# A two-block layer on one core: block products of a triangular inversion in separate bursts, transfers handed out when their data are there, low maps first, two output units begun early

## The chip, the cores and the metric

The kernel runs on one core of a Trainium2 chip. The metric is the device time of one execution in microseconds (us); smaller is better. Engines: PE = TensorE matmul, PEld = TensorE weight load, DVE = VectorE, ACT = ScalarE, POOL = GpSimd, SP = SyncE, which issues most transfers.

## The reference

Two transformer-like blocks over 512 tokens of width 1024. The change touches the mixer of the second block alone: an RWKV-7 recurrence and a gated depthwise convolution of 31 taps, each followed by an output map and merged by two gates. Cut to that:

```python
def rwkv7_time_mix(h, p_r, p_k, p_v, ...):
    xx = token_shift(h) - h
    r, k, v = (lerp_shift(p, mu) for p, mu in zip((p_r, p_k, p_v), mu_rkv))
    w_log = -softplus(-(w0 + tanh((h + xx * mu_wag[0]) @ w1) @ w2)) - 0.5
    decay = exp(-exp(w_log))
    a = sigmoid(a0 + ((h + xx * mu_wag[1]) @ a1) @ a2)
    g = sigmoid((h + xx * mu_wag[2]) @ g1) @ g2
    kk = heads(k * kk_scale) / norm                     # 16 heads of 64
    y = wkv7(r, decay, k * (1 + (a - 1) * ka_scale), v, -kk, kk * a)
    y = group_norm(y) * gn_w + gn_b
    return ((y + bonus * v) * g) @ w_o

def wkv7(r, w, k, v, a, b):                             # per head, over the tokens
    S = S * w + (S @ a) b^T + v k^T
    y = S @ r

def conformer_conv(p_c, ...):
    u, gate = split(p_c)
    c = depthwise_conv31(u * sigmoid(gate)) + dw_b
    return silu(layer_norm(c)) @ w_o

merged = sigmoid(z_rwkv) * y_rwkv + sigmoid(z_conv) * y_conv
x = x + rms_norm(merged @ w_out); x = x + ffn(x)
```

## The kernel before

Outside the mixer the program is a sequence of dense stages. The mixer is the **drive stage** (`drive`, L1712, 1276 to 2029 us of the trace). Activations are kept transposed, in a high and a low half (`hT_h`, `hT_l`; three products of halves stand for one fp32 product), and so are the weights: ACT writes the high half `wh` of a loaded `raw` block, and DVE or POOL writes the low half `wl` (`wsplit`). A **dense unit** (`dense`, L1063) is one 128-column block of a weight matrix against 512 tokens: for 8 slices k the products `hT_h,wh` and `hT_l,wh`, 16 matmuls, then 8 of `hT_h,wl`, 24 in all into one PSUM bank. The units run in a list (L1637): `i0`..`i7`, one per pair of heads (three projections r, k, v, and the *low map*, which multiplies the low-rank activations `lo` for decay, rate and gate), `c0`..`c7` (convolution inputs), `g0`..`g15` (gates, `gate` L1165), `w0`..`w7` (RWKV output map, which needs the finished rows), `m0`..`m7` (convolution output map). A projection ends in an ACT pass and a DVE pass from its bank into `rkv` (the lerp); the low map takes three banks.

Beside the units run **streams**, Python generators that emit small pieces between two pieces of a unit:
- `outs` (L1648): per pair the decays, the scaled keys, and the chunk products (`pair_out`, L1175).
- `solves` (L1660): per group of two pairs the inversion (`solve`, L1300) of the 64 x 64 triangular blocks of 32 chunk-heads. 8 x 8 blocks on the diagonal are solved by substitution on DVE (buffers `at`, `tt`, moved through DRAM `ab`, `td` to change their layout); the results `dd` and `dt` (its transpose, by DVE) are then widened to 32 and 64 by block products on TensorE. One such product is a **quad** (`quad`, L1316): 64 matmuls of 32 x 32.
- `chains` (L1675): the recurrence over 8 chunks (`chain`, L1428), state `SV`.
- `posts` (L1683): group norm, bonus and gate of a group's rows (`post`, L1469; `bv` is the bonus from DRAM); behind the third, the six finished rows are loaded as `yv` and split into halves; the last group's two rows are split in `post`.
- `ends` (L1700): the layer norm of the convolution (`layer_norm`, L1550): `asum`, then DVE and ACT passes over the eight maps `xc` for the sum of squares `ssum`, then two passes a map for its result `ct_h`, `ct_l`.
- The convolution's taps (`conv`, L1512) fill DVE: `acc` is a map's sum.

A **planner** sets the order: while the program is written, `Clock` (L88) keeps a time for each engine from costs (`cost`, L122; `op`, L134), and `burst` (L1715) gives every stream whose due time has come its next piece. What a stream yields tells its due time: `BURST` and `FREE` wait for the last result, `WAIT` asks again at the next piece, `LAZY` goes by DVE's time; `stand` (L1733) moves the clock on when no unit may begin. The order so written holds on PE and DVE. Instructions written in the drive stage carry L151 (L191 for matmuls) in the trace, those elsewhere L185.

Two places that the change cuts open, first the second and third level of the inversion (L1364 to L1390), two quads back to back:

```python
pa, pb = quad(of(de), of(dd)), quad(of(dd), of(de))
```

and the start of the output map, whose units all wait for the last group:

```python
return [(lambda: wraw(wcols(G2("w_rwkv_out"), 0, KD, f * P, P), KD, P), wsplit, run, lambda: posts_done == 4)]
```

Of the kernel before, what the change touches and what calls it, by code (L numbers as in the profile page):

```python
# [13 lines left out]
F32 = mybir.dt.float32  # L14
# [8 lines left out]
P = 128  # L23
# [64 lines left out]
class Clock:  # L88
# [45 lines left out]
    def op(self, engine, op, out, ins, f, a, k):  # L134
# [7 lines left out]
        if op == "dma_start":  # L142
            end += 3.0
# [72 lines left out]
def tile_two_blocks(ctx: ExitStack, tc: tile.TileContext, A, out):  # L216
# [782 lines left out]
    with ExitStack() as es:  # L999
# [63 lines left out]
        def dense(hl, xh=lambda k: hT_h[:, k, :], xl=lambda k: hT_l[:, k, :], cut=KD):  # L1063

            (h, l), ps = hl, pst()
            n = 0
            for ks in (range(cut), range(cut, KD)):
                for part in range(2):
                    for k in ks:
                        if part:  # L1070
                            nc.tensor.matmul(ps, lhsT=l[:, k, :], rhs=xh(k), start=False, stop=k == KD - 1)
                        else:
                            nc.tensor.matmul(ps, lhsT=h[:, k, :], rhs=xh(k), start=k == 0, stop=False)
                            nc.tensor.matmul(ps, lhsT=h[:, k, :], rhs=xl(k), start=False, stop=False)
                        n += 2 - part
                        if n % 2 == 0 and n < 3 * KD:
                            yield n % 8 != 0
            return ps


        def pair_in(j):
# [6 lines left out]
            def proj(i):  # L1088
# [3 lines left out]
                def run(hl):  # L1092
# [8 lines left out]
                    nc.vector.scalar_tensor_tensor(to, o, der[:, i, j : j + 1], to, ALU.mult, ALU.add)  # L1101
                    yield
# [15 lines left out]
            def run(hl):  # L1118
# [16 lines left out]
                R.done = True  # L1135
# [37 lines left out]


        def pair_out(j, G):  # L1175
# [101 lines left out]
            for s in range(2):  # L1277
# [15 lines left out]
                yield FREE  # L1293
            R.grams, L.grams = True, False
# [5 lines left out]
        def solve(g, G):  # L1300
# [6 lines left out]

            def d32(t, i):

                return bass.AP(t.tensor, t.offset + 16 * i * 1024, [[32, 32], [1024, 16], [1, 32]])  # L1310
# [23 lines left out]
            for i in range(4):  # L1334
                nc.sync.dma_start(d32(ab, i), diag[i])
            yield
# [3 lines left out]
            pr = x[:, 256:]  # L1340
            e = s2("e")
# [8 lines left out]

            nc.gpsimd.memset(tt, 0.0)
            nc.gpsimd.memset(tt.rearrange("p m a b -> p m (a b)")[:, :, ::9], 1.0)
            for r in range(4):
                nc.sync.dma_start(at[64 * (r // 2) : 64 * (r // 2) + 64, r % 2], d8(ab, r))
            yield
# [7 lines left out]
            yield  # L1363
# [3 lines left out]
            yield  # L1367
# [14 lines left out]
            pb, pa = quad(of(dd), of(de)), quad(of(de), of(dd))  # L1382
# [5 lines left out]
            dT, rr = s2("dT"), s2("rr")  # L1388
            nc.scalar.activation(dT, pa, AF.Copy)
# [22 lines left out]
            for n in range(4):  # L1412
# [12 lines left out]
                nc.vector.tensor_copy(G.RB[:, jj, cc, :], ps[:, :, 1])  # L1425
# [43 lines left out]
        def post(g, G, dst=None):  # L1469
# [21 lines left out]
            yield  # L1491
# [20 lines left out]
        def conv():  # L1512
# [8 lines left out]

            for f in range(KD):
                while f >= len(convs):
                    yield False
# [3 lines left out]
                for t in range(1, 31):  # L1528
# [3 lines left out]
                    if t > 9 and f + 1 == len(begun) and f + 1 < len(convs):  # L1532
                        begin(f + 1)
# [66 lines left out]

        def rwkv_map(f):
            def run(hl):
                if f == 0:
                    L.cm = big_tile("X1", [P, KD, T])
                z = zload(0, f)
                ps = yield from dense(hl, L.yT_h, L.yT_l)
                nc.vector.tensor_tensor(L.cm[:, f, :], ps, z, ALU.mult)
                yield
            return [(lambda: wraw(wcols(G2("w_rwkv_out"), 0, KD, f * P, P), KD, P), wsplit, run, lambda: posts_done == 4)]

        def conv_map(f):
# [9 lines left out]
            def keep(raw):  # L1621
                if f == 0:
                    L.wo = [[big_tile(n, [P, 2, 1, D], F32R) for n in nn] for nn in (("SV1", "BKT1"), ("RA0", "RA1"))]
                ready[f + 4] = wsplit(raw, [t[f // 2][:, f % 2] for t in L.wo])

            out = [(lambda: wraw(wcols(G2("w_conv_out"), 0, KD, f * P, P), KD, P), wsplit, run, lambda: ln_done)]
            if f < 4:
                out.append((lambda: wraw(wcols(G2("w_out"), f + 4, 1, 0, D), 1, D), keep, None, None))
# [3 lines left out]
        CCB, WAIT, BURST, FREE, LAZY, SPLIT = 2, "wait", "burst", "free", "lazy", 3  # L1632
        L, ready, pairs, groups, convs = Ctx(), {}, {}, {}, []
        solves_done = chains_done = posts_done = 0
        ln_done, L.convs, L.decay, L.grams = False, 0, False, False
# [173 lines left out]
```

## Time and profile before

| | us |
|---|---|
| median of 3 runs | 2447.92 |
| fastest, slowest | 2445.57, 2455.46 |
| profiled execution, its own time | 2455.02 |
| its span | 2453.2 |
| TensorE busy | 2319.7 (95%) |
| VectorE busy | 1191.4 (49%) |
| ScalarE busy | 953.1 (39%) |
| mean granted TensorE clock | 0.971 |

The profile is of one execution; times in it count from its span's start. A row of a timeline is a run of like instructions: start, duration, engine, line, operation, output <- input with shapes, count, and in brackets the idle time of the engine ahead of it with what ended that. "issue" stands where nothing that the profile records ended it. A matmul of fp32 operands is two in the trace. [...]

### The profile page before, as it was taken

The page shows a single profiled execution, that of the slowest core. Times are in us where ns is not written, and L with a number is a line of the kernel's source. Part 1 is how long each engine was busy: PE and PEld are TensorE (multiplying, and loading weights), DVE is VectorE, ACT ScalarE, POOL GpSimd, SP SyncE. Part 2 cuts the span into 40 slices and gives each one's busy share as a digit, 9 for nine tenths or more (in the row PEclk, how much of TensorE's full clock was granted, in tenths as well). Part 3 has the DMA queues.
Part 4 walks back from the last instruction along what each step waited for, and adds up shares of the span by engine and source line. Part 5 has one row for each costly group of instructions (what it writes and reads, how often), then busy time and mean ns, then how long its engine had stood idle before and what let it go on. Part 6 is the DMA issues. An engine that isn't in the chain of part 4 may idle for free. (4 is left out here: it accounts for less than half of the span.)

```text
span 2453.2 us, 38288 instructions
## 1 busy us (share of the span) xinstructions
PE 2319.7 (95%) x15723; PEld 1869.3 (76%) x15723; DVE 1191.4 (49%) x1846; ACT 953.1 (39%) x1721; POOL 347.3 (14%) x463
## 2 busy tenths in 40 slices
PE   8899999999999999999999988998987889999998
PEld 6755888888787788888887776777765667888886
DVE  4376532233433653223446756767757665422232
ACT  4355432133343552222245554564532343322221
POOL 1000120000100000000024323433423221000000
PEclk9989999999999999999999989999999899999999
DMA  7320763233532153332233322232334244433231
GB/s 203 106 79 26 201 203 102 62 117 116 163 111 87 61 164 106 97 101 95 69 103 100 81 62 73 81 82 83 108 100 155 81 152 165 143 99 95 95 97 58
DMA packets 326287, 262.60 MB, mean 107 GB/s; under 512 B 46896, under 2 KB 293748, under 8 KB 325728
## 3 DMA queue, kind: packets, MB, share of 16 engines
q1 hardware_dynamic: 308296, 211.18, 29.4%
q10 hardware_dynamic: 9080, 22.37, 3.1%
q0 software_dynamic: 8736, 26.61, 3.1%
q8 instruction: 123, 2.02, 0.3%
q14 instruction: 52, 0.43, 0.1%
HBM read 225.81 MB, written 34.31 MB: 106 GB/s over the span
## 5 line engine op out<-in xcount | busy, mean ns | idle before, releaser
L185 PE MATMUL p<-hT_h,wh 128*128 128x512 f32 (+1 forms) x1376 | 511.5, 377 | 7.9 <-ACT qT L185 6.0
L185 DVE TENSOR_TENSOR wl<-raw,wh 128x1024 fp32r<-128x1024 f32 (+1 forms) x270 | 319.3, 1187 | 398.6 <-ACT wh L185 349.4
L185 PE MATMUL p<-hT_l,wh 128*128 128x512 f32 (+1 forms) x1376 | 511.1, 376 | 0.0
L185 ACT ACTIVATE wh<-raw 128x1024 fp32r<-128x1024 f32 (+1 forms) x270 | 275.9, 1026 | 548.8 <-PE p L185 374.1
L185 PE MATMUL p<-hT_h,wl 128*128 128x512 f32 (+1 forms) x1376 | 328.1, 376 | 0.0
L185 PEld LDWEIGHTS p<-hT_h,wh 128*128 128x128 f32 x1376 | 260.3, 189 | 56.1 <-ACT qT L185 6.4
L185 PEld LDWEIGHTS p<-hT_l,wh 128*128 128x128 f32 x1376 | 260.6, 189 | 46.7 <-issue 0.6
L185 PEld LDWEIGHTS p<-hT_h,wl 128*128 128x128 f32 x1376 | 248.4, 189 | 46.6 <-DVE wl L185 0.4
L185 POOL TENSOR_SCALAR rstd<-ss 128x1 f32<-128x1 f32 x52 | 17.7, 340 | 1460.2 <-ACT junk L185 1460.0
L151 DVE SCALAR_TENSOR_TENSOR acc<-c,dwc,acc 128x512 f32<-128x512 f32 x240 | 209.2, 873 | 7.1 <-ACT acc L151 0.9
L185 PE MATMUL p<-wh,fh 128*128 128x512 f32 x528 | 206.2, 390 | 1.6 <-ACT memv L185 0.9
L185 PE MATMUL p<-wl,fh 128*128 128x512 f32 x528 | 206.1, 390 | 0.0
L185 PE MATMUL p<-wh,fl 128*128 128x512 f32 x528 | 205.5, 390 | 0.0
L191 PE MATMUL p<-hT_h,wh 128*128 128x512 f32 x448 | 190.0, 424 | 0.7 <-ACT hn L185 0.7
L191 PE MATMUL p<-hT_l,wh 128*128 128x512 f32 x448 | 181.7, 406 | 0.0
L185 DVE TENSOR_TENSOR fT<-sg,p 128x384 f32<-128x384 f32 (+1 forms) x88 | 46.7, 552 | 257.0 <-PE p L185 250.4
L191 PE MATMUL p<-hT_h,wl 128*128 128x512 f32 x448 | 123.5, 420 | 7.9 <-DVE wl L151 7.9
L151 ACT ACTIVATE wh<-raw 128x1024 fp32r<-128x1024 f32 x78 | 77.2, 990 | 110.0 <-PE p L191 78.4
L151 POOL TENSOR_TENSOR wl<-raw,wh 128x1024 fp32r<-128x1024 f32 x39 | 97.6, 2504 | 151.6 <-PE p L191 51.4
L185 PEld LDWEIGHTS p<-wh,fh 128*128 128x128 f32 x528 | 99.2, 188 | 22.6 <-ACT memv L185 1.3
L185 DVE TENSOR_TENSOR fl<-fT,fh 128x512 fp32r<-128x512 f32 x66 | 45.1, 691 | 145.1 <-ACT fh L185 145.1
L185 PEld LDWEIGHTS p<-wl,fh 128*128 128x128 f32 x528 | 99.2, 188 | 20.5
(304 smaller groups left out, 3554.4 us busy)
## 6 DMA issues: line engine op xcount, KB each, us to landing
raw<-in_w_gu SPq DMA_DIRECT2D x88, 512.0 KB
raw<-in_w_in SPq DMA_DIRECT2D x56, 512.0 KB
raw<-in_w_down SPq DMA_DIRECT2D x44, 512.0 KB
raw<-in_ffn_w_gate SPq DMA_DIRECT2D x22, 512.0 KB
raw<-in_ffn_w_up SPq DMA_DIRECT2D x22, 512.0 KB
raw<-in_ffn_w_down SPq DMA_DIRECT2D x22, 512.0 KB
raw<-in_w_in_b SPq DMA_DIRECT2D x20, 512.0 KB
xs<-xt POOLq DMA_DIRECT2D x19, 512.0 KB, 3.9
```

The costliest lines, as they stand in the source:

```text
L151: return f(*a, **k)
L185: return f(*a, **k)
L191: return f(*a, **k)
```

## The change

1. *Separate bursts*: where the inversion issued two quads back to back, the second now stands behind a `yield FREE`, in both levels; a copy of each pair goes from DVE to ACT, as does the copy into `RB`.
2. *Transfers when the data are there*: a new stream helper `there(x)` yields `WAIT` until the planner's PE time is within 0.3 us of the time at which x is ready. The inversion uses it ahead of each of its transfers and passes; its first transfers move to `pair_out`, after each pair's chunk products; `bv` and the gates in `post`, and the stored convolution maps (`stored`), are handed out later likewise. The planner's costs of a transfer change.
3. *Low maps first*: the low map becomes the first of a pair's four units; the unit list changes to `c6 g0 i6 c7 i7`.
4. *Two output units begun early*: `w0` and `w1` run their slices k = 0..5 once the six first rows are split (`L.rows == 6`), then `HOLD` until the last group is done, then k = 6, 7. The loads of the six rows become a stream of their own (`mapped_rows`). The four `w_out` blocks are loaded in w3, w6, m1, m4 instead of m0 to m3.

```diff
     def cost(self, engine, op, out, ins):
...
-            return 0.65 if engine == "POOL" else 0.05
+            n, wide = math.prod(out.shape), len(out.shape) > 2 and out.shape[-1] < P
+            return 0.65 if engine == "POOL" else 0.4 if not wide else 0.8 if n == 8192 else 0.65
...
-            end += 3.0
+            end += 2.5 if math.prod(out.shape) < P * 4 * P else 3.5 if math.prod(out.shape) < P * P * 8 else 5.0
...
-            return [(*proj(i), lambda: j < 2 or hasattr(pairs[j - 2], "out")) for i in range(3)] + [(load, cut_, run, None)]
+            return [(*u, lambda: j < 2 or hasattr(pairs[j - 2], "out")) for u in ((load, cut_, run), *map(proj, range(3)))]
...
+        def there(x):
+
+            yield WAIT
+            while clock.free("PE") < clock.ready(x) - 0.3:
+                yield WAIT
...
+            for i in range(4):
+                nc.sync.dma_start(d32(abd[j // 2 % 2], i, 8 * jj, 8), AB[32 * i : 32 * i + 32, jj, :, 32 * (i % 2) : 32 * (i % 2) + 32])
             R.grams, L.grams = True, False
...
-            for i in range(4):
-                nc.sync.dma_start(d32(ab, i), diag[i])
-            yield
...
+            yield from there(ab)
...
-            yield
+            yield from there(td)
             dd, dt = s2("dd"), s2("dt")
             for i in range(4):
                 nc.sync.dma_start(dd[q32(i)], d32(td, i))
-            yield
+            yield from there(dd)
             nc.vector.transpose(dt, dd)
             yield BURST
...
-            pa, pb = quad(of(de), of(dd)), quad(of(dd), of(de))
-            dd, dt = s2("dd"), s2("dt")
-            nc.vector.tensor_copy(dt, pb)
-            nc.scalar.activation(dd, pa, AF.Copy)
+            dd_, dt = s2("dd"), s2("dt")
+            nc.scalar.activation(dt, quad(of(dd), of(de)), AF.Copy)
+            yield FREE
+            nc.scalar.activation(dd_, quad(of(de), of(dd)), AF.Copy)
+            dd = dd_
             yield BURST
             de = s2("de")
             nc.scalar.activation(de, quad(lambda i: diag[i], of(dt), True), AF.Copy)
             yield BURST
-            pb, pa = quad(of(dd), of(de)), quad(of(de), of(dd))
+            pb = quad(of(dd), of(de))
...
+            yield FREE
+            dT = s2("dT")
+            nc.scalar.activation(dT, quad(of(de), of(dd)), AF.Copy)
...
+            yield
+            for jj in range(2):
                 nc.sync.dma_start(gt[jj], gd[2 * g + jj])
...
         def rwkv_map(f):
+            first, rest = range(6), range(6, KD)
...
+                ps = yield from dense(hl, L.yT_h, L.yT_l, first)
+                if f == 0:
+                    L.held = ps, hl
+                    return
+                yield HOLD
+                for f_, ps, hl in ((0, *L.held), (1, ps, hl)):
+                    finish(f_, (yield from dense(hl, L.yT_h, L.yT_l, rest, ps)))
...
+            if f in (3, 6):
+                out.append(load_out((f - 3) // 3))
...
-        for what in ("c0 i0 i1 c1 i2 i3 c2 c3 i4 c4 i5 c5 i6 c6 i7 c7 "
+        for what in ("c0 i0 i1 c1 i2 i3 c2 c3 i4 c4 i5 c5 c6 g0 i6 c7 i7 "
...
+        def mapped_rows():
+            while not L.rows:
+                yield WAIT
+            for f in range(6):
+                yv = lnp.tile([P, T], F32, tag="yv", name="yv", bufs=2)
+                nc.sync.dma_start(yv, yd[f])
+                yield
+                split(L.yT_h(f), L.yT_l(f), yv)
+                yield LAZY
+            L.rows = 6
...
+                    if at_ == HOLD:
+                        while posts_done < 4:
+                            stand()
```

TensorE's order in the second level of the first group's inversion. `dt,e`, `dd,de` and `de,dd` are quads, `lo` the low map, `hT_h`, `hT_l` dense units, `X,bk` the chunk products of a pair. Before:

```order
L191 MATMUL p_10758<-dt,e 32x32 x64
L191 MATMUL p_10827<-lo,wh 128x512 x2
L191 MATMUL p_10827<-lo,wl 128x512
L191 MATMUL p_10828<-lo,wh 128x512 x2
L191 MATMUL p_10828<-lo,wl 128x512
L191 MATMUL p_10839<-dd,de 32x32 x64
L191 MATMUL p_10904<-de,dd 32x32 x64
L191 MATMUL p_10973<-lo,wh 128x512 x2
```

The change:

```order
L192 MATMUL p_10820<-hT_l,wh 128x512
L192 MATMUL p_10924<-X_10556,bk 128x128 x4
L192 MATMUL p_10933<-X_10556,bk 128x128 x4
L192 MATMUL p_10941<-ident,rkv 128x128 x4
L192 MATMUL p_10948<-blk,so 128x2 x4
L192 MATMUL p_10955<-ident,rkv 128x128 x4
L192 MATMUL p_10964<-de,dd 32x32 x64
L192 MATMUL p_10820<-hT_h,wl 128x512 x8
L192 MATMUL p_11051<-X_10556,bk 128x128 x4
L192 MATMUL p_11059<-X_10556,bk 128x128 x4
L192 MATMUL p_11067<-dd,de 32x32 x64
L192 MATMUL p_11137<-hT_h,wh 128x512
```

The second quad now stands behind eight dense matmuls and the chunk products of the next pair; the low map is gone from here.

TensorE's order at the end of the last chain, up to the first dense matmuls of the output map (`SV,X`, `RA,SV`: last chain step; `RA,blk`, `blk,RA`, `ident,RA`: the group norm's centring, sums and spreading; `asum,oneD`, `oneD,ssum`, `ident,asum`: the layer norm's mean, its variance and its spreading). Before:

```order
L191 MATMUL p_16573<-RA_14374,SV_13683 64x64 x4
L191 MATMUL p_16592<-RA_14374,blk 128x512
L191 MATMUL p_16596<-RA_14374,blk 128x512
L191 MATMUL p_16604<-blk,RA_14374 128x2 x4
L191 MATMUL p_16612<-blk,RA_14374 128x2 x4
L191 MATMUL p_16627<-ident,RA_14374 128x128 x4
L191 MATMUL p_16636<-ident,RA_14374 128x128 x4
L191 MATMUL p_16659<-X_16132,wh 128x512
```

The change:

```order
L192 MATMUL p_16650<-RA_14477,SV_13826 64x64 x4
L192 MATMUL p_16669<-RA_14477,blk 128x512
L192 MATMUL p_16673<-RA_14477,blk 128x512
L192 MATMUL p_16681<-asum,oneD 128x512
L192 MATMUL p_16684<-blk,RA_14477 128x2 x4
L192 MATMUL p_16691<-blk,RA_14477 128x2 x4
L192 MATMUL p_16733<-oneD,ssum 128x2 x4
L192 MATMUL p_16740<-ident,RA_14477 128x128 x4
L192 MATMUL p_16746<-ident,RA_14477 128x128 x4
L192 MATMUL p_16761<-ident,asum 128x128 x4
L192 MATMUL p_16530<-X_16380,wh 128x512
```

The layer norm's three products have moved into this place, its variance ahead of the group's spreading; the first dense matmul behind it is that of the slices k = 6, 7. DVE in the same place, the change (`RA_14477` and `BKT` are the group's rows, `RA_16389`, `xc` and `acc` the maps of the layer norm; before, six taps `acc<-c,dwc,acc` stood between the reductions and the first `RA<-RA,p`):

```order
L152 TENSOR_TENSOR acc<-acc,asum 128x512
L152 TENSOR_TENSOR ssum<-ssum,sq 128x512 x2
L152 TENSOR_SCALAR r_16738<-p_16733 128x8
L152 TENSOR_TENSOR RA_14477<-RA_14477,p_16740 128x512
L152 TENSOR_TENSOR RA_14477<-RA_14477,p_16746 128x512
L152 TENSOR_TENSOR RA_14477<-RA_14477,bv 128x512
L152 TENSOR_TENSOR RA_14477<-RA_14477 128x512
L152 TENSOR_TENSOR RA_16389<-RA_16389,p_16761 128x512
L152 TENSOR_TENSOR RA_14477<-RA_14477,bv 128x512
L152 TENSOR_TENSOR RA_16389<-RA_16389,p_16761 128x512 x2
L152 TENSOR_TENSOR ct_l<-RA_16389,ct_h 128x512
L152 TENSOR_TENSOR RA_14477<-RA_14477 128x512
```

The passes of the sums stand ahead of the group's own, and the first of the norm's second half among them.

## Rows read from the trace of the kernel before

**Rows 1.** The page: busy time of each engine (part 1), the queue of instructions (part 3).
```profile
PE 2319.7 (95%) x15723; PEld 1869.3 (76%) x15723; DVE 1191.4 (49%) x1846; ACT 953.1 (39%) x1721; POOL 347.3 (14%) x463
...
q8 instruction: 123, 2.02, 0.3%
```
**Rows 2.** Windows: feed-forward stretch; end of the drive stage; sum over its eight windows.
```profile
1165.27:1226.60 61.33, 61.33 (x272) 50.82 (x271) 25.49 (x27) 17.04 (x22) 0.00 (x0) 1.00 0.23 69
1923.00:2029.00 106.00, 94.71 (x387) 74.76 (x388) 64.49 (x77) 42.50 (x54) 26.66 (x11) 0.95 0.43 134
...
sum 753.00, PE 672.83 PEld 526.54 DVE 506.69 ACT 363.34 POOL 258.29; mean PE 84.10 PEld 65.82 DVE 63.34 ACT 45.42 POOL 32.29
```
**Rows 3.** Waits of PE in the drive stage: us in total, times, longest.
```profile
PE p L191 <- issue: 24.5, 11, 3.3
PE p L191 <- DVE wl L151: 14.6, 5, 7.9
PE p L191 <- DVE SV L151: 9.5, 8, 3.3
PE p L191 <- DVE rkv L151: 6.9, 4, 3.3
PE p L191 <- ACT wh L151: 6.6, 3, 2.8
PE p L191 <- DVE dt L151: 4.7, 2, 2.9
```
**Rows 4.** Timeline of PE, two quads of the first group's inversion.
```profile
1411.18 1.24 PE L191 MATMUL p<-dd,de 32*32 32x32 f32 x123
1415.75 0.27 PE L191 MATMUL p<-dd,de 32*32 32x32 f32 x3 [3.33 <-issue]
...
1415.85 1.84 PE L191 MATMUL p<-de,dd 32*32 32x32 f32 x121
1419.50 0.32 PE L191 MATMUL p<-de,dd 32*32 32x32 f32 x5 [1.81 <-issue]
```
**Rows 5.** Windows: the stretches of quads of the four groups.
```profile
1405.00:1440.00 35.00, 27.47 (x844) 21.54 (x843) 15.34 (x24) 19.87 (x30) 10.28 (x10) 0.80 0.21 64
1505.00:1530.00 25.00, 18.90 (x766) 14.64 (x752) 15.65 (x23) 7.63 (x15) 5.83 (x10) 0.86 0.19 57
1664.00:1690.00 26.00, 20.15 (x709) 15.69 (x710) 18.40 (x25) 8.62 (x12) 7.08 (x7) 0.87 0.34 118
1785.00:1812.00 27.00, 21.36 (x776) 16.39 (x776) 15.29 (x22) 6.42 (x12) 2.37 (x4) 0.85 0.12 34
```
**Rows 6.** Timeline of PE at a low map's third product; window around it.
```profile
1329.75 1.22 PE L191 MATMUL p<-lo,wh 128*128 128x512 f32 x2 [3.26 <-DVE rkv L151]
...
1325.00:1340.00 15.00, 11.74 (x50) 9.08 (x49) 11.24 (x14) 10.20 (x16) 8.40 (x7) 0.77 0.40 128
```
**Rows 7.** Timelines of DVE and PE ahead of the last chain.
```profile
1844.12 0.69 DVE L151 TENSOR_TENSOR RA<-RA,bv 128x512 f32<-128x512 f32 x1 [3.59 <-DMA bv<-bvd]
...
1864.18 3.78 PE L191 MATMUL p<-hT_h,wl 128*128 128x512 f32 x8 [7.87 <-DVE wl L151]
```
**Rows 8.** Waits of SP's queue in the drive stage, the largest.
```profile
SPq L151 <- DVE wl L151: 198.6, 31, 25.3
```
**Rows 9.** Timelines of PE and DVE at the end of the last chain.
```profile
1904.25 1.01 PE L191 MATMUL p<-RA,SV 64*64 64x64 f32 x8 [0.33 <-ACT SV L151]
...
1915.78 0.78 PE L191 MATMUL p<-X,wh 128*128 128x512 f32 x1
...
1922.95 0.75 PE L191 MATMUL p<-BKT,wh 128*128 128x512 f32 x1 [2.17 <-DVE BKT L151]
...
1911.27 4.68 DVE L151 SCALAR_TENSOR_TENSOR acc<-c,dwc,acc 128x512 f32<-128x512 f32 x6
```
**Rows 10.** Timeline of DVE, first and last rows of the layer norm's sums (15 passes).
```profile
1932.94 1.90 DVE L151 TENSOR_TENSOR RA<-RA,asum 128x512 f32<-128x512 f32 x3 [4.89 <-ACT asum L151]
...
1941.81 2.63 DVE L151 TENSOR_TENSOR ssum<-ssum,sq 128x512 f32<-128x512 f32 x1 [0.15 <-ACT sq L151]
```

More of the change, by code (lines that the diff above doesn't have):

```diff
@@ L1061, in chunks, with dense @@
             return t.rearrange("p (c t) -> p c t", t=C)
-        def dense(hl, xh=lambda k: hT_h[:, k, :], xl=lambda k: hT_l[:, k, :], cut=KD):
-            (h, l), ps = hl, pst()
+        def dense(hl, xh=lambda k: hT_h[:, k, :], xl=lambda k: hT_l[:, k, :], ks=range(KD), ps=None):
+            h, l = hl
+            ps = pst() if ps is None else ps
             n = 0
[L1067 to L1077, printed above, removed]
+            for part in range(2):
+                for k in ks:
+                    if part:
+                        nc.tensor.matmul(ps, lhsT=l[:, k, :], rhs=xh(k), start=False, stop=k == KD - 1)
+                    else:
+                        nc.tensor.matmul(ps, lhsT=h[:, k, :], rhs=xh(k), start=k == 0, stop=False)
+                        nc.tensor.matmul(ps, lhsT=h[:, k, :], rhs=xl(k), start=False, stop=False)
+                    n += 2 - part
+                    if n % 2 == 0 and (n < 3 * len(ks) or len(ks) < KD):
+                        yield n % 8 != 0
             return ps
@@ L1340, in solve @@
             pr = x[:, 256:]
+            nc.gpsimd.memset(tt, 0.0)
+            nc.gpsimd.memset(tt.rearrange("p m a b -> p m (a b)")[:, :, ::9], 1.0)
+            yield from there(ab)
+            for r in range(4):
+                nc.sync.dma_start(at[64 * (r // 2) : 64 * (r // 2) + 64, r % 2], d8(ab, r))
             e = s2("e")
@@ L1349, in solve @@
                 nc.scalar.activation(diag[i][:, :, 16:], diag[i][:, :, 16:], AF.Copy, scale=blk[q32(i), P : P + 1])
[L1351 to L1354, printed above, removed]
-            yield
+            yield from there(at)
             for t in range(1, 8):
@@ L1520, in begin, with stored @@
                 begun.append((c, acc))
+            def stored(f):
+                return clock.free("PE") > clock.ready(cd[f]) - 0.5
             for f in range(KD):
                 while f >= len(convs):
+                    yield False
+                while f == len(begun) and not stored(f):
                     yield False
@@ L1694, in posts @@
                     L.yT_h, L.yT_l = cat(yh[:, :4], yh[:, 4:]), halves("SV0", "BKT0")
[L1695 to L1698 removed]
+                    L.rows = True
+        def mapped_rows():
[4 more added lines that the diff above has]
+                nc.sync.dma_start(yv, yd[f])
+                yield
+                split(L.yT_h(f), L.yT_l(f), yv)
+                yield LAZY
+            L.rows = 6
+            yield WAIT
         def ends():
@@ L1740, in drive @@
             hl, idle = units[0][1](raws.pop(0)), 0.0
-            for i, (_, _, run, pre) in enumerate(units):
+            for i, (_, _, run, pre, *_) in enumerate(units):
                 t = clock.free("PE")
@@ L1748, in drive @@
                 nxt, more = None, i + 1 < len(units)
-                for n, minor in enumerate(run(hl) if run is not None else ()):
-                    if n == SPLIT and more:
+                for n, at_ in enumerate(run(hl) if run is not None else ()):
+                    if at_ == HOLD:
+                        while posts_done < 4:
+                            stand()
+                    if more and (at_ == SPLIT or (n == 3 and not units[i][4:])):
                         nxt, more = units[i + 1][1](raws.pop(0)), False
-                    burst(minor)
+                    burst(at_ is True)
                     taps.until(clock.free("PE") - 1)
```

66 lines of the change are left out of this document (37 added, 29 removed).

## The prediction

> **What bounds it now.** I read the page's first part first: TensorE is busy for 2319.7 of 2453.2 us [rows 1], so only its idle stretches and its slow clock can be won. The change leaves everything outside the recurrent mixer (1276 to 2029 us) as it was, so next I cut that stretch by windows: TensorE is busy 672.8 of 753.0 us and so idle for 80; from 1923 on its granted clock is 0.95, while the feed-forward stretch ahead, without a wait, shows 1.00 and 272 dense matmuls in 61.33 us, 0.23 us each [rows 2]. Then who ended the waits [rows 3]: 24.5 us have no releaser ("issue"), 14.6 are low weight halves, 9.5 the chain's state `SV`, 6.9 the lerp's result `rkv`, 6.6 high halves, 4.7 the transposed `dt`. Each group was then looked up in the timelines.
>
> The 24.5 us lie inside the quad products of the inversion. One quad is 64 matmuls in the order and 128 in the trace, since these are fp32. Between the resumptions at 1415.75 and 1419.50 stand 3+2+2+121 = 128 matmuls with as many weight loads, they need 2.0 us, and 3.75 us pass [rows 4]. The instruction queue brought 123 packets of 2.02 MB, 16 KB each; 15723 matmuls and as many loads over 123 are 256 instructions a packet [rows 1]. So I read these waits as code that had not arrived: 256 TensorE instructions that run in under about 3.75 us have to wait for the next packet. Two quads back to back are 512 instructions in 2.5 us.
>
> [...]
>
> **The change, part by part.** TensorE runs the same matmuls before and after (the order), so only waits and clock move. A fall of the clock to its lower level is priced as (1 - granted clock) x length.
>
> *Products in separate bursts.* In the new order each of the eight former second quads has other work ahead of it, in seven cases eight dense matmuls, in one six of the low map. I cut the new order into blocks of 256 instructions from the same starting point and priced each by the trace (0.23 us a dense matmul [rows 2], 0.01 one of a quad, 123 in 1.24 [rows 4], the rest likewise). Twelve to sixteen blocks are still short, because eight dense matmuls are only 1.9 us. With 3.75 us a block they lack 15 us together, with 3.5 us 11, with 4.5 us 27; the same count on the old order gives 27 where the trace has 24.5. I take 14: 10.5 us won. The four stretches of quads lose 7.0, 3.5, 3.4 and 4.1 us by the clock, 18 in all [rows 5]; with the waits about two fifths shorter I take 6. Together **-16.5** (bounds -24 and +5).
>
> *Low maps first.* The three products of `lo` take three PSUM banks within 2 us, and the third needs the bank of the unit just ended. Before, that was always the pair's value projection, read by an ACT pass and then by a DVE pass in DVE's order. Waits: 6.9 us on `rkv` [rows 3] and 2.3 on a late low half (of the 14.6 of rows 3, 7.9 stand in rows 7 and 4.5 behind 1923), 9.2 in all. After, six of eight low maps follow a gate or a convolution unit whose bank needs one more pass, of ACT or DVE; two still follow the value projection of another pair. I keep 2 us. Three of these waits lie in a stretch of 15 us at 0.77, of which one stands in [rows 6], 3.4 us each; I take 8 of 10. **-15** (bounds -5, -19).
>
> *Transfers handed out when their data are there.* The two waits on `dt` (4.7 us [rows 3]) stood behind a DVE transpose that waited for a DMA; the new wait lets only this stream stand while dense units run on. I take -4, and -1.5 of clock. At 1844.12 DVE had waited 3.59 us for the second `bv`, then for a `yv`; behind these a low half came late and TensorE stood 7.87 us, its next eight matmuls taking 3.78 us where 0.23 each makes 1.9 [rows 7]. With the longest `SV` wait, 3.3 us just ahead [rows 3], that is 11.2 us, of which 1 stays: the new order puts chain steps between the load and its use, and loads `yv` in a stream of its own. -10, clock -2.5. Together **-18** (bounds -6, -20). SyncE issues 16 more transfers (523 to 539, the order); its queue stood mostly for freed weight buffers, 199 us on DVE alone [rows 8], so this costs nothing. If that slack were gone, weights would be late.
>
> *Two output units early, and the tail.* This part speaks against the change. The 36 matmuls begun early only shift work. But in the new order TensorE has nothing dense between the last chain step and the last group's finished rows, and the whole statistics part of the layer norm now stands there, on DVE ahead of the group's own normalisation and on TensorE ahead of its transposes. Before: last chain product at 1904.25, dense again at 1915.78 with the rows that were split already, then a stop of 2.17 us until 1922.95 for the last two rows [rows 9]; 11.5 + 2.2 = 13.7 us bare, with six taps of 4.68 us on DVE inside [rows 9]. The norm's sums ran under dense matmuls, 15 passes from 1932.94 to 1944.4 [rows 10]. After: nothing dense before the point that was 1922.95, 18.7 us behind the chain, and 22 DVE passes (15 of the sums, one reduction, six of the norm's second half) take the place of the six taps. At the pitch of the sums, 14 passes in 8.87 us [rows 10], that is 22 x 0.63 - 4.7 = 9.2 us; I add 3, an estimate, for the squares that wait behind the group's expansions on ACT, and 1 for the sums' own matmul. That makes 32 us, 18 more than 13.7; less 2, since the clock's recovery in this place is paid once now and was paid twice. **+16** (bounds +5, every new pass hidden, and +32: the second half's other ten passes inside, 6 us, and five passes as slow as the 2.63 of rows 10, 10 us).
>
> *Behind the tail.* Because the norm is over early and the four `w_out` loads are spread over w3, w6, m1 and m4 instead of m0 to m3, I expect most of the 6.6 us on high halves [rows 3] and the 4.5 on low halves to go: -9, and -3 of the 5.3 us of clock [rows 2]. **-12** (bounds -3, -14).
>
> *New waits.* One more chain step is bare of dense work, +2; two `yv` loads share ACT with the chain, +1. Some 30 of the 80 us idle have causes that no part aims at, and in a new order they may grow; I add a third, 10. **+13** (bounds 0, +25). Sixteen copies go from DVE to ACT and six low halves from POOL to DVE; DVE, busy 507 of 753 us [rows 2], takes both unseen.
>
> Sum: -16.5 - 15 - 18 + 16 - 12 + 13 = -32.5 us, against the profiled execution's 2455.0. That run is 7 us over the median of 2447.92, and the same terms from the median give **2415 us**.
>
> **Rivals.** (1) *The forecast*, 0.50: 2398 to 2438. (2) *Fetch stays*: more single crossings instead of a few double ones, each still with its fall of the clock. For it: the twelve to sixteen short blocks. Against it: the shortfall halves on paper. The term goes to zero, or to +5 by its bound: 2432 to 2437; 0.17. (3) *All relieved*: tail at +5, no new waits: 2415 - 11 - 13 = 2391 and less, to 2380; 0.10. (4) *The order does not matter*: the planner's times are guesses before and after, so each wait removed comes back elsewhere. For it: those 30 us, and that three of the waits that go are DVE's order. Against it: the fetch and bank waits are structural. 2448 give or take 8; 0.12. (5) *The tail decides, slower*: place, the end of the last chain; price +32 by its bound; new waits +25; together +57. It decides once the parts ahead and behind give less than 45 of the 61.5 us that I expect of them. With these at their lower ends (0, -5, -6, -3) the change is +43, with fetch and banks as forecast +16: 2464 to 2491; 0.11.
>
> **Numbers.** About 0.5%, 12 us, is what a measurement can tell from no change. Faster, under 2436, takes (1), (3), over half of (2) and a little of (4): 0.70. Same is the rest of (2) and most of (4): 0.17. Slower is (5) and the edge of (4): 0.13. The range leaves out the lower half of (3) and (5): 2388 to 2456.
>
> **What would show it.** Right: "issue" falls from 24.5 to 10 to 18 us in shorter pieces; waits on `rkv` fall under 3 us, on `dt` under 1.5; no wait of 7 us on a low half near the last chain; the tail is bare for about 32 us instead of 13.7, with the sums on DVE inside; the 100 us behind it have under 4 us of waits on weights. Wrong: "issue" at 20 or more, a tail over 45 us, or over 20 us of waits on DVE that the old profile does not have.

## The result and the profile after

The change takes 2429.85 us (median of 6 runs, 2426.35 to 2435.73) against 2446.74 before (6 runs, 2444.65 to 2455.46): ratio 0.9917, 95% interval 0.9899 to 0.9936, so some 20 us (16 to 25) faster. By the medians it is 17 us. The profiled execution took 2429.3 us, near its median; that of before had 2455.0, some 8 over its own. So the two traces differ by 25.7 us of span, more than the runs do, and sizes are taken from the runs where they can be.

The page's busy times, then the drive stage by windows (its stretch up to the last chain product, the tail up to the second dense matmul behind it, and the rest; a row gives start and end, length, then what the head of the view names, PEclk being TensorE's granted clock as a share of full speed):

```profile
PE 2313.3 (95%) x15723; PEld 1862.5 (77%) x15723; DVE 1198.5 (49%) x1832; ACT 965.3 (40%) x1743; POOL 339.0 (14%) x457
```

```profile
core 0: us, PE busy (x) PEld busy (x) DVE busy (x) ACT busy (x) POOL busy (x), PEclk, DMA share, GB/s
1280.16:1882.33 602.17, 563.53 (x7201) 439.80 (x7201) 444.90 (x666) 326.14 (x625) 220.84 (x262) 0.97 0.33 96
1882.33:1915.50 33.17, 12.42 (x52) 8.35 (x52) 20.52 (x35) 17.79 (x29) 6.45 (x4) 0.56 0.09 24
1915.50:2002.95 87.45, 84.61 (x347) 67.80 (x348) 48.09 (x50) 31.35 (x37) 22.52 (x9) 0.95 0.51 157
sum 722.79, PE 660.56 PEld 515.95 DVE 513.51 ACT 375.28 POOL 249.81; mean PE 220.19 PEld 171.98 DVE 171.17 ACT 125.09 POOL 83.27
```

The drive stage ran from 1275.84 to 2028.62 before, with 672.45 us busy for 7598 matmuls, and now takes 722.8 us, 660.6 busy for as many. Of the 30.0 us between the profiled executions 18.1 are idle time (80.3 to 62.2). The other 11.9 are busy time for the same matmuls, which is read as the clock: by windows over the whole stage, 0.93 was granted before and 0.95 now. The stage starts 4.3 us later, with nothing changed ahead of it; that and the 8 us say how far two single executions may differ, and e3 below shows a difference as large inside the stage. A third of the idle time that is left, 20.8 of 62.2 us, stands in the 33 us of the tail.

PE's waits in the stage (us in total, times, longest), beside [rows 3], with two of before behind them:

```profile
PE p L192 <- DVE ssum L152: 12.3, 1, 12.3
PE p L192 <- DVE RA L152: 10.6, 9, 3.1
PE p L192 <- DVE SV L152: 7.2, 6, 4.0
PE p L192 <- issue: 6.4, 6, 2.3
PE p L192 <- DVE BKT L152: 5.4, 1, 5.4
PE p L192 <- DVE wl L152: 5.4, 2, 2.8
PE p L192 <- DVE rkv L152: 3.0, 2, 2.4
```

```profile
PE p L191 <- DVE RA L151: 4.1, 5, 1.4
PE p L191 <- DVE BKT L151: 2.2, 1, 2.2
```

"issue" went from 24.5 to 6.4, low halves from 14.6 to 5.4, `rkv` from 6.9 to 3.0; `dt` and the high halves are gone. Two waits of the tail are new or have grown, `ssum` (12.3) and `BKT` (from 2.2 to 5.4), and `RA` has grown from 4.1 to 10.6. Over all waits, those that fell come to some 47 us and those that rose or are new to some 28.

Four quads of the first group's inversion in PE's timeline, beside [rows 4]: each runs its 128 matmuls without a stop.

```profile
1435.12 1.46 PE L192 MATMUL p<-de,dd 32*32 32x32 f32 x128
1441.87 1.29 PE L192 MATMUL p<-dd,de 32*32 32x32 f32 x128
...
1454.51 1.50 PE L192 MATMUL p<-de,dd 32*32 32x32 f32 x128
1458.44 1.58 PE L192 MATMUL p<-dd,de 32*32 32x32 f32 x128
```

The tail on PE, from the last chain product to the second dense matmul, beside [rows 9]:

```profile
1882.33 0.77 PE L192 MATMUL p<-RA,SV 64*64 64x64 f32 x8 [0.32 <-ACT SV L152]
...
1901.81 1.87 PE L192 MATMUL p<-oneD,ssum 128*128 128x2 f32 x8 [12.29 <-DVE ssum L152]
...
1909.27 0.79 PE L192 MATMUL p<-X,wh 128*128 128x512 f32 x1 [1.70 <-ACT X L152]
1915.48 0.80 PE L192 MATMUL p<-BKT,wh 128*128 128x512 f32 x1 [5.42 <-DVE BKT L152]
```

From 1882.33 to 1915.48 it is 33.15 us, against 11.5 + 2.2 before. TensorE first waits 12.3 us for the norm's squares, then for what the group's own rows need behind them. DVE makes the sums there, and waits for the squares itself:

```profile
1889.67 1.90 DVE L152 TENSOR_TENSOR RA<-RA,asum 128x512 f32<-128x512 f32 x3
1894.20 0.69 DVE L152 TENSOR_TENSOR ssum<-ssum,sq 128x512 f32<-128x512 f32 x1 [2.63 <-ACT sq L152]
```

And the low maps' new neighbours, on PE among the first three pairs; the last row is of before:

```profile
1345.32 1.87 PE L192 MATMUL p<-blk,so 128*128 128x2 f32 x8 [3.14 <-DVE RA L152]
...
1363.50 0.50 PE L192 MATMUL p<-hT_h,wh 128*128 128x512 f32 x1 [1.96 <-ACT ls L152]
...
1391.31 0.94 PE L192 MATMUL p<-lo,wh 128*128 128x512 f32 x2 [2.35 <-DVE rkv L152]
...
1401.85 3.69 PE L192 MATMUL p<-hT_h,wl 128*128 128x512 f32 x8 [2.61 <-DVE wl L152]
```

```profile
1384.71 1.22 PE L191 MATMUL p<-lo,wh 128*128 128x512 f32 x2 [2.32 <-DVE rkv L151]
```

Before, this place had waits of 3.26 [rows 6] and 2.32 us on `rkv`. Now the unit behind the low map waits 1.96 us for `ls`, the ACT pass that reads the low map's bank, and one wait of 2.35 us on `rkv` stays: 4.3 us for 5.6. With the waits on `RA` and on a low half the stretch is no better: its first 129 us are idle for 11.9 us, where it was 9.5.

### The profile page after: what moved, and what is told of

Read it like the earlier page. It is cut to its first block, busy times and chain, and to the rows that moved or that the text cites. A ratio compares the mean times of both kernels' runs of the same rounds, so it can differ in the third digit from the quotient of the medians.

```text
span 2427.5 us, 38347 instructions
## 1 busy us (share of the span) xinstructions
PE 2313.3 (95%) x15723; PEld 1862.5 (77%) x15723; DVE 1198.5 (49%) x1832; ACT 965.3 (40%) x1743; POOL 339.0 (14%) x457
## 5 line engine op out<-in xcount | busy, mean ns | idle before, releaser
L186 ACT ACTIVATE wh<-raw 128x1024 fp32r<-128x1024 f32 (+1 forms) x270 | 275.8, 1025 | 547.6 <-PE p L186 370.6
L186 POOL TENSOR_SCALAR rstd<-ss 128x1 f32<-128x1 f32 x52 | 18.6, 358 | 1467.0 <-ACT junk L186 1466.8
L152 ACT ACTIVATE wh<-raw 128x1024 fp32r<-128x1024 f32 (+1 forms) x78 | 77.4, 992 | 114.2 <-PE p L192 57.3
L186 PEld LDWEIGHTS p<-wh,fl 128*128 128x128 f32 x528 | 99.1, 188 | 20.4
```

Of the source, the lines that this page charges most:

```text
L152: return f(*a, **k)
L186: return f(*a, **k)
```

## The experiments

The theory to be tried: waits without a releaser are code that comes in blocks of 256 TensorE instructions, as the author worked out from [rows 1] and [rows 4], the waits on `rkv` are for a PSUM bank, the rest of the gain is DVE standing for transfers; the norm in the tail costs some 16 us. Rivals: the waits are data that the profile doesn't show; or the parts are not worth what their waits show, because a planned order only moves them. The runs were made on several chips, so all ratios are to the kernel before on the same chip, beside the change's 0.9917; a hundredth is 24 us. e9, behind the table, was run once, for its trace.

| run | edit | ratio (95%) |
|---|---|---|
| e1 | change, quads together | 1.0011 (0.9997 to 1.0024) |
| e2 | change, low maps last | 0.9994 (0.9978 to 1.0011) |
| e4 | change, part of the transfer edits undone | 0.9937 (0.9918 to 0.9956) |
| e10 | change, all transfer edits undone | 0.9933 (0.9912 to 0.9954) |
| e3 | change, norm behind the last group | 0.9889 (0.9871 to 0.9906) |
| f3 | e3, no early units | 0.9896 (0.9868 to 0.9923) |
| f4 | e3, `w_out` loads in m0 to m3 | 0.9900 (0.9871 to 0.9928) |
| e7 | before, separate bursts alone | 0.9996 (0.9978 to 1.0015) |
| e8 | before, low maps first alone | 0.9983 (0.9969 to 0.9998) |
| f1 | e7, norm behind the last group | 0.9940 (0.9916 to 0.9963) |
| f2 | f1, low maps first as well | 0.9964 (0.9947 to 0.9982) |

### Is it code? Half a block more ahead (e9)

```diff
                 ps = pst()
+                if not shifted:
+                    shifted.append(1)
+                    for _ in range(32):
+                        nc.tensor.matmul(ps[:32, :32], lhsT=ident[:32, :32], rhs=ident[:32, :32], start=True, stop=True,
+                                         tile_position=(0, 0))
```

> The kernel before with 32 more small matmuls of the identity at the very start of the program, where TensorE waits anyway: 64 matmuls and 64 weight loads in the trace, half of 256; their result is overwritten. Everything else keeps its order. Theory, code comes in blocks of 256 TensorE instructions: each stop without a releaser stands 64 matmuls earlier in the order than before (or 64 later); the first group's stop behind 123 matmuls of dd,de stands behind 59 of them. Rival, a wait on data or on a semaphore that the profile does not show: the stops stand at the same matmuls as before.

PE's timeline of this run at the place of [rows 4]:

```profile
1414.11 0.72 PE L191 MATMUL p<-dd,de 32*32 32x32 f32 x60
1415.92 0.76 PE L191 MATMUL p<-dd,de 32*32 32x32 f32 x66 [1.09 <-issue]
...
1419.39 0.79 PE L191 MATMUL p<-de,dd 32*32 32x32 f32 x68 [2.18 <-issue]
```

And the stop of the next pair of quads, before and in this run:

```profile
1435.07 0.84 PE L191 MATMUL p<-dd,de 32*32 32x32 f32 x42 [2.25 <-issue]
```

```profile
1434.42 1.65 PE L191 MATMUL p<-dd,de 32*32 32x32 f32 x106 [2.47 <-issue]
```

The stop behind 123 matmuls of `dd,de` now stands behind 60 (the counts are those of the records, of which some are missing), 64 earlier but for one; in the next pair of quads 106 matmuls are left behind the stop where 42 were, 64 more. Of the eleven stops of before, ten have moved by 64 matmuls, to within one, earlier or later. The eleventh, of 0.62 us, is gone, and two of 1.02 and 0.76 us are new. The total is 23.0 us where it was 24.5. Apart from the matmuls at the start, order, data and semaphores are the same in both kernels, so the stops belong to the place in the code: shown. That TensorE waits there for code that has not arrived is the author's reading; the records name nothing.

### Each part undone in the change (e1, e2, e4, e10)

e1 takes the two `yield FREE` out:

```diff
             nc.scalar.activation(dt, quad(of(dd), of(de)), AF.Copy)
-            yield FREE
             nc.scalar.activation(dd_, quad(of(de), of(dd)), AF.Copy)
...
-            yield FREE
             dT = s2("dT")
```

> The change, but the two quads of each of the two levels are written back to back again (the two FREE yields are taken out; who copies is left as in the change). Theory, code that has not arrived: the waits without a releaser go from 6.4 us in the change back to 20 to 27, at pairs of quads and at multiples of 256 TensorE instructions, and with the clock behind them the time goes up by 12 to 24 us, to 2442 to 2454. Rival, the new order only happens to be better there and the separation returns nothing: waits without a releaser under 10 us, time within 4 us of the change (2426 to 2434).

2452.39 us median. Its waits:

```profile
PE p L192 <- issue: 23.1, 15, 2.4
PE p L192 <- DVE SV L152: 17.7, 13, 4.2
PE p L192 <- DVE ssum L152: 10.5, 1, 10.5
```

There are 16.7 us more without a releaser and 10.5 more on `SV`. The stage is idle for 80.3 us instead of 62.2 and busy for 672.9 instead of 660.6, so 12.4 us of busy time come beside 18.1 of idle time in these two traces. The theory held; the whole gain hangs on this part.

e2 puts the low map last again and restores the unit list:

```diff
-            return [(*u, lambda: j < 2 or hasattr(pairs[j - 2], "out")) for u in ((load, cut_, run), *map(proj, range(3)))]
+            return [(*u, lambda: j < 2 or hasattr(pairs[j - 2], "out")) for u in map(proj, range(3))] + [(load, cut_, run, None)]
...
-        for what in ("c0 i0 i1 c1 i2 i3 c2 c3 i4 c4 i5 c5 c6 g0 i6 c7 i7 "
-                     + " ".join(f"g{n}" for n in range(1, 16)) + " " + " ".join(f"w{n}" for n in range(8)) + " "
+        for what in ("c0 i0 i1 c1 i2 i3 c2 c3 i4 c4 i5 c5 i6 c6 i7 c7 "
+                     + " ".join(f"g{n}" for n in range(16)) + " " + " ".join(f"w{n}" for n in range(8)) + " "
```

> The change, but the low map is the last of a pair's four units again and the unit list is the old one. Theory, the bank of the value projection: waits on rkv ahead of the low map's third product go from 3.0 us back to 6 to 9, with a late low half of some 2 us and the clock behind them: 8 to 15 us more, 2438 to 2445. Rival, the wait only moved from one product to another: within 4 us of the change, since the first products of the low map now wait instead.

2448.38 us median, beyond what was expected. Its waits:

```profile
PE p L192 <- DVE rkv L152: 17.1, 8, 4.4
PE p L192 <- DVE SV L152: 14.9, 6, 4.3
PE p L192 <- ACT X L152: 14.6, 1, 14.6
```

In this order the waits on `rkv` cost 17.1 us, two and a half times what they cost before the change. `ACT X` is the tail, with the second half of the norm in it. The trace is of the slowest of its twelve runs, 9 us over their median.

e4 makes `there` a plain yield and loads the rows in `posts`; e10 also puts back the first transfers of `solve`, those of `post` and `conv`, and the planner's costs:

```diff
         def there(x):
 
-            yield WAIT
-            while clock.free("PE") < clock.ready(x) - 0.3:
-                yield WAIT
+            yield
```

Of e10 beside this, its costs and its first transfers:

```diff
-            return 0.65 if engine == "POOL" else 0.4 if not wide else 0.8 if n == 8192 else 0.65
+            return 0.65 if engine == "POOL" else 0.05
...
-            end += 2.5 if math.prod(out.shape) < P * 4 * P else 3.5 if math.prod(out.shape) < P * P * 8 else 5.0
+            end += 3.0
...
+            for i in range(4):
+                nc.sync.dma_start(d32(ab, i), diag[i])
+            yield
```

> The change, but there(x) is one plain yield (due when the last result is, the transfer not counted), and the six finished rows are loaded and split in one go by the stream of the posts again. Theory, DVE stands for a transfer and what queues behind it is late: waits on dt of 3 to 5 us return, and one of 5 to 8 us on a low half or on SV in the stretch of the last two chains, 8 to 16 us more, 2438 to 2446. Rival, these waits were taken by other edits (the place of bv, the costs of a transfer): within 4 us of the change.

> The change without any of its edits on transfers: there(x) a plain yield, the rows loaded by the stream of the posts, the inversion's first transfers at its start, the gates and the bonus of the post and the stored convolution maps handed out as before, and the planner's old costs of a transfer. Theory, as predicted, these edits are worth some 18 us: waits on dt of 3 to 5 us and one of 5 to 8 us on a low half come back, 2440 to 2450. Rival, from the run with a part of them undone: the waits they aimed at went with the new order, within 5 us of the change, 2426 to 2436.

2432.24 and 2438.8 us median, by the ratios 4 to 5 us over the change, with intervals that overlap the change's. By its median e10 lies just above what the rival had and just below what the theory had; by its ratio it is with the rival. Of their waits, e4 then e10:

```profile
PE p L192 <- DVE SV L152: 15.3, 10, 5.2
```

```profile
PE p L191 <- DVE SV L151: 12.1, 10, 4.2
```

No wait on `dt` came back in either, none of 5 us or more on a low half; e4 has one of 5.2 us on `SV` in the last chain, where the change has 4.0. `SV` as a whole rose from 7.2 to 15.3 and 12.1 us, "issue" from 6.4 to 9.5 and 11.6. The rival held: these waits went with the new order. e8, below, says the same, with the old transfers and none of the two waits.

### The norm in the tail (e3, f3, f4)

```diff
         def ends():
             nonlocal ln_done
-            while L.convs < KD - 1 or lnp is None or posts_done < 3:
+            while L.convs < KD - 1 or lnp is None or posts_done < 4:
                 yield WAIT
```

> The change, but the layer norm may only begin when the last group is done (one number, 3 becomes 4). Theory, the 12.3 us wait of TensorE on ssum is the price of the norm's statistics in the tail: from the last chain product to the second dense matmul behind it 33 us become 18 to 20, and the sums run under the output units; 11 to 15 us less than the change, 2415 to 2419. Rival, the norm is then late for the convolution's output map, or its passes hold up low halves on DVE: waits of 8 us or more on ct_h, ct_l or wl behind the tail, and the time within 4 us of the change.

2421.16 us median. PE at the tail:

```profile
1880.11 1.02 PE L192 MATMUL p<-RA,SV 64*64 64x64 f32 x8 [0.32 <-ACT SV L152]
...
1895.11 0.80 PE L192 MATMUL p<-X,wh 128*128 128x512 f32 x1 [2.87 <-ACT X L152]
1898.71 0.80 PE L192 MATMUL p<-BKT,wh 128*128 128x512 f32 x1 [2.81 <-DVE BKT L152]
```

The tail is 18.6 us, 14.5 shorter, as expected. But the time fell by 7 us by the ratios and 8.7 by the medians, not 11 to 15. The stage up to the tail, the tail and the stretch behind it, to be set beside the windows of the change:

```profile
1270.11:1880.11 610.00, 568.08 (x7200) 443.28 (x7200) 446.48 (x664) 326.01 (x625) 221.80 (x262) 0.96 0.33 95
1880.11:1898.71 18.60, 11.03 (x38) 7.21 (x38) 8.28 (x14) 6.59 (x11) 4.57 (x3) 0.51 0.16 43
1898.71:1998.10 99.39, 89.98 (x361) 70.16 (x362) 57.40 (x73) 42.39 (x55) 24.06 (x10) 0.94 0.44 138
```

Behind the tail TensorE is idle for 9.4 us where it was 2.8, and runs the norm's three products there: this stretch grows by 11.9 us. So in these two traces an early norm gives back four fifths of what it costs, and by the ratios of the runs about half. The traces cannot say more, since up to the tail TensorE's order is the same in both kernels, matmul for matmul, and yet this part took 610.0 us in one and 602.2 in the other, while the part ahead of the stage, the same too, took 10 us less in e3's. The five runs of e3 (2420.4 to 2425.0) lie below all six of the change (2426.4 to 2435.7), though the intervals of the two ratios just touch; it beats the kernel before clearly and the change by a little.

From this kernel, f3 lets no unit begin early and f4 has the loads late:

```diff
-            out = [(lambda: wraw(wcols(G2("w_rwkv_out"), 0, KD, f * P, P), KD, P), wsplit, run, lambda: posts_done == 4 or f < 2 and L.rows == 6, *([SPLIT] if f == 1 else []))]
+            out = [(lambda: wraw(wcols(G2("w_rwkv_out"), 0, KD, f * P, P), KD, P), wsplit, run, lambda: posts_done == 4, *([SPLIT] if f == 1 else []))]
```

```diff
-            if f in (3, 6):
-                out.append(load_out((f - 3) // 3))
...
-            if f in (1, 4):
-                out.append(load_out(2 + (f - 1) // 3))
+            if f < 4:
+                out.append(load_out(f))
```

> The change with the layer norm held until the last group is done, and w0 and w1 not begun early. Theory of the prediction, the 36 matmuls only shift work: within 4 us of the same kernel with early units (2421 us). Rival, they fill the last chain steps, where TensorE has nothing else: bare time there grows by some 6 to 8 us (36 matmuls of 0.23 us are 8.3), 2426 to 2430.

> The change with the layer norm held until the last group is done, and the four w_out loads in m0 to m3 as before. Theory of the prediction: waits on high halves in the convolution's output map come back, 6 to 7 us, with clock 7 to 11 us more than the same kernel with spread loads (2421 us), 2428 to 2432. Rival, the loads then no longer collide with the norm's passes in w3 and w6, and the waits of 2 to 3 us there go: within 3 us.

2423.51 and 2425.09 us median. The early units only shift work, as the prediction had it, as far as the intervals tell. The loads are worth some 3 to 4 us by ratio and median, and that is not told from nothing: f4 has 6.0 us of waits on high halves where e3 has 3.0, half of what was expected.

### Parts alone, on the kernel before (e7, e8, f1, f2)

e7 takes the quads' hunks of the change, e8 those of the low map:

```diff
-            pa, pb = quad(of(de), of(dd)), quad(of(dd), of(de))
...
+            nc.scalar.activation(dt, quad(of(dd), of(de)), AF.Copy)
+            yield FREE
+            nc.scalar.activation(dd_, quad(of(de), of(dd)), AF.Copy)
```

```diff
-            return [(*proj(i), lambda: j < 2 or hasattr(pairs[j - 2], "out")) for i in range(3)] + [(load, cut_, run, None)]
+            return [(*u, lambda: j < 2 or hasattr(pairs[j - 2], "out")) for u in ((load, cut_, run), *map(proj, range(3)))]
```

> The kernel before with one part of the change alone: the two quads of each of the two levels in separate bursts, with the copies as in the change. Theory, code that has not arrived: waits without a releaser fall from 24.5 us to 6 to 10, and with the clock behind them the time falls by 14 to 24 us, to 2424 to 2434. Rival, parts are not independent, the old order gives it back (the low maps stand between the quads there and now wait elsewhere): within 6 us of before.

> The kernel before with one part of the change alone: the low map as the first of a pair's four units, and the new unit list. Theory, the bank of the value projection: waits on rkv fall from 6.9 us to 2 to 4, and with a late low half and the clock the time falls by 8 to 18 us, to 2430 to 2440. Rival: the low maps also stood between the quads of the old order as cover for their code; without them the waits without a releaser grow by 4 to 10 us and the time stays within 6 us of before.

Next to nothing from either: 2451.27 and 2451.3 us, where before had 2452.55. The waits of e7, then of e8:

```profile
PE p L191 <- DVE SV L151: 15.4, 10, 6.3
PE p L191 <- issue: 11.9, 9, 3.6
PE p L191 <- DVE rkv L151: 11.4, 5, 4.5
PE p L191 <- DVE RA L151: 11.2, 10, 3.1
PE p L191 <- DVE ssum L151: 10.3, 1, 10.3
```

```profile
PE p L191 <- issue: 22.9, 11, 3.9
PE p L191 <- DVE SV L151: 15.0, 15, 4.8
...
PE p L191 <- DVE rkv L151: 3.2, 2, 2.5
```

In e7 "issue" is halved, but the convolution's taps end earlier, and the norm, which waits for them, falls into the tail. The last taps begin 8.5 us behind the last chain product (1902.40 and 1893.91), where before it was 20.5 (1924.73 and 1904.25). So TensorE waits 10.3 us on `ssum`, which the kernel before doesn't have. In e8 `rkv` falls as expected; `SV` rises by 5.5. f1 and f2 take the norm out of the tail, by the edit of e3; f2 has both parts:

> The kernel before with separate bursts, and the layer norm held until the last group is done. Theory, the separate bursts alone gave nothing because the norm's statistics then fell into the tail (TensorE waited 10.3 us on ssum and 6.8 on asum there): without these the 12.6 us that they save on code show, 8 to 16 us less than before, ratio 0.9935 to 0.9967. Rival, it was the waits on rkv, RA and SV that took their place: ratio 0.998 or more.

> The kernel before with separate bursts and the low maps first, and the layer norm held until the last group is done; no edits on transfers, no early units, w_out loads as before. Theory, each of the two parts needs the other (undone one by one each takes the whole gain away): ratio 0.989 to 0.993, with under 10 us without a releaser and under 4 us on rkv. Rival, the gain needs the early units, the loads or the transfers too: ratio 0.995 or more.

f1 is 0.6% faster than before, 2435.02 us, as expected: the bursts' gain had been hidden by the tail. The edit of e3 on the kernel before alone was not run; there the sums run from 1932.94 on [rows 10], already behind the group's last rows. f2, with the low maps too, is at 2442.15, no faster than f1: the rival held. "issue" is 7.9 us there, and `rkv` 2.3, as expected; but `SV` is 21.2, and one low half came late, on PE and on DVE:

```profile
1485.61 3.78 PE L191 MATMUL p<-hT_h,wl 128*128 128x512 f32 x8 [8.72 <-DVE wl L151]
```

```profile
1474.43 9.99 DVE L151 SCALAR_TENSOR_TENSOR acc<-c,dwc,acc 128x512 f32<-128x512 f32 x8
1484.34 1.22 DVE L151 TENSOR_TENSOR wl<-raw,wh 128x1024 fp32r<-128x1024 f32 x1
```

The planner put eight taps, 10 us, ahead of a low half whose high half ACT began at 1474.08. A reason may be that with the old costs of a transfer the planner believed the input late and filled DVE up to then; that was not tried by itself. f4 and f2 differ by the transfer edits, the early units and the engine that copies into `RB`, and by 0.64%, where e10 and the change differ by 0.16%. So what those edits are worth depends on the order they meet, and stays open.

## Why the prediction was right, and where its terms were not

The time lies in the range (2388 to 2456) and in that of the forecast itself, case (1) of its rivals, faster as forecast, at five to six tenths of the gain: 20 us by the ratio, or 17 by the medians, where the sum had 32.5. That the total came so near is in part luck. Taken apart another way, the sum has -9.5 us of waits (-10.5 - 7 - 14 + 18 - 9 + 13) and -23 us of clock (-6 - 8 - 4 - 2 - 3). The two traces show -18.1 of idle time and -11.9 of busy time, so the waits won twice as much as forecast and the clock half. Step by step:

- **Separate bursts, -16.5.** Right, and too small. The count by blocks gave 14 us left; 6.4 were left. Undone, it is worth 0.94%, some 23 us (e1). That the stops keep to a place in the code is shown by e9: 64 matmuls more at the start moved ten of eleven by 64 matmuls, to within one, as blocks of 256 instructions (128 matmuls with their loads) would have it. With nothing for this term the sum would have ended 16 us higher, near 2431, which is where the time did end; but the runs do not bear that out, since the stops cost 23 to 25 us in each of three kernels with back-to-back quads (24.5 before, 23.1 in e1, 23.0 in e9), and e1 puts the time back.
- **Low maps first, -15.** The wait was read rightly and mis-sized as a gain. `rkv` fell by 3.9 us and the late low half of 2.3 went, but among the first pairs 1.96 us on `ls`, 3.14 on `RA` and 2.61 on a low half came in. The step that failed is "six of eight low maps follow a gate or a convolution unit whose bank needs one more pass": it counted who waits for the bank ahead of the low map and not who waits for the low map's own three banks. Alone it is worth 0.17% (e8), 4 us; undone in the change it costs 19, with 14.1 us more on `rkv`.
- **Transfers, -18.** The step that failed. Both waits went, but they go without these edits too (e4, e10, e8): 4 to 5 us in the change. The prediction credited the edit that named the transfer; the new orders that were tried broke up the row of waits `bv`, `yv`, low half without it. What it said of DVE's order in rival (4) was right here.
- **Tail, +16.** Right to about 1 us in its main number: 32 us bare forecast, 33.15 measured, with the sums' passes from 1889.67 on inside and 2.63 us of wait for the squares where 3 was allowed. That it adds 16 us to the time was too much taken by itself: e3 returns 7 to 9, since the early norm pays for the stretch behind.
- **Behind the tail, -12.** Waits on weights there fell from 11.1 to 2.8 us, 8.3 of the 9 forecast. With the norm behind they are 7.0 us with the spread loads (e3) and 12.1 with the late ones (f4), so in these traces the two causes that the term named, the early norm and the loads, share this about evenly; in time the loads are not told from nothing (f4). Tail and this term belong together: +4 by the sum, +7 to 9 by the runs of e3, and +2.6 by its trace.
- **New waits, +13.** About right: `RA` +6.5, `BKT` +3.2, `ls` 2.1, `X` 1.7 us, 13.5 together, of which 5.1 are those counted under the low maps. One sign named for being wrong, over 20 us of waits on DVE that the old profile does not have, came up on the way: `ssum`, `RA`, `BKT` and `r` have 22.6 us more. But 12.3 of them are `ssum`, which the tail's term had priced.

What the sum had wrong beyond sizes is that its terms were added. Each of the two main parts alone gives next to nothing, and each undone takes all; a planner's order answers an edit elsewhere, in e7 by when the taps end and so where the norm falls. Why the low maps are worth 19 us in the change and nothing on f1 stays open.

## What to carry to other kernels

Small matmuls in a row can stop at a fixed count of instructions, as the quads did here, 3.5 to 3.75 us from one stop to the next, 128 matmuls on ([rows 4], e9): look for stops without a releaser, shift the code by half that count to see whether they move, and put other work between the bursts. In a kernel whose order is planned, price an edit by undoing it in the new order as well as by making it alone, and look first at what moved into the stretch with the fewest things to do, as the norm did here. A stretch where the busiest engine stands bare is worth a rule of its own (e3: one number, 7 to 9 us). And a stage's length from one trace is not yet a size: the same TensorE order took 602 us in one and 610 in another.

## What was not expected of the hardware

It took little to make the stops without a releaser cheap. Six stops of 6.4 us remain of eleven of 24.5, where the count by 3.75 us a block gave 15. In part there is more between two quads than the eight dense matmuls (1.9 us) that the count had: in the two pairs shown above the quads begin 6.8 and 3.9 us apart. Where a second block follows at once, as in e9, TensorE runs 128 matmuls from one stop to the next (1415.92 and 1419.39, 3.5 us; 3.75 in [rows 4]).

The 7598 matmuls of the stage took from 660.6 (the change, at a granted clock of 0.95) to 681.7 us (e8, at 0.92) of busy time in the profiled executions. How much of that an order decides stays open: up to the tail the same order was busy for 563.5 us in the change's trace and for 568.1 in e3's.
